# A five-branch decoder layer: the last product's pieces on two PSUM tiles, and one quarter of the last normalization

## Chip, cores and metric

The kernel runs on one core of one Trainium2 chip. The metric is the time of one execution on the device, in microseconds (us): the median of three runs of each kernel. Before the change it is 469.82 us (469.64 to 471.61).

## What is computed

One post-norm decoder layer over 256 tokens of width 1024. Five branches (block attention, a dilated-window mixture, forgetting attention, a gated delta rule, and cross-attention into 256 memory tokens) read the same input; each is gated, projected to width 1024 and merged under a sigmoid. What the change touches is the last of it:

```python
y = jnp.sum(jax.nn.sigmoid(merge_logits) * y, axis=2)   # (1, 256, 1024)
y = y @ w_out                                            # 1024 x 1024
return _layer_norm(DEEPNORM_ALPHA * x + y, ln_g, ln_b)

def _layer_norm(x, g, b):
    mu = x.mean(-1); var = square(x - mu).mean(-1)
    return (x - mu) * rsqrt(var + 1e-5) * g + b
```

All of it is float32. Each product is made of three matmuls: both operands are split into a rounded part (`hi`, by ScalarE) and a remainder (`lo`, by VectorE), and hi·hi, hi·lo and lo·hi are added up in PSUM (`mm3`, line 128 of the profile).

## The kernel before

The kernel goes through a list of weight units. Each unit loads a piece of a weight by DMA (line 176), splits it (lines 123 and 124) and multiplies it; small steps of the attention branches are dealt in between. The order on each engine is set when the kernel is built, by a scheduler that works from the program's order and a model of the time, and semaphores are set where one engine needs another's result.

The last product, `y @ w_out`, is done in `out_units`. Its output has two halves of 128 tokens, t = 0 and t = 1. They are cut into five **pieces** (`PC`): t = 0 into columns 0 to 511 (piece 0) and 512 to 1023 (piece 1); t = 1 into 0 to 511 (piece 2), 512 to 767 (piece 3) and 768 to 1023 (piece 4). Each piece adds up in its own PSUM space over 8 blocks of w_out's rows, k = 0 to 7. The blocks k = 0, 1, 2 are multiplied as they come, for all pieces in turn. The other five are kept back (`late`), and `finish` then multiplies them piece by piece: 15 matmuls for piece 0, 15 for piece 1, and so on. When a piece is complete, VectorE adds the residual to it and writes it to SBUF (line 1071, here called the eviction), and takes its mean and variance (line 1072). After the last piece of a half, `norm(t)` normalizes it: the statistics are brought together (1055), ScalarE takes a square root (1058), VectorE takes the reciprocal (1059), and for each half of the columns, c = 0 and 1, VectorE makes two passes over 128x512 elements (1062: subtract the mean, times g; 1063: times the reciprocal, plus b). Column half 0 then leaves by a DMA from SyncE's queue, column half 1 by one from ScalarE's queue (1064).

The PSUM space of the pieces: two tiles `lg` of two 512-column halves each, and one tile `mm` of 512 columns. Before the change pieces 0 and 1 are the two halves of the first `lg` tile (lg_6037 in the order below), pieces 2 and 3 those of the second (lg_6038), and piece 4 lies in `mm` (mm_6039). `big` in the profile is here the residual stream `xres`, written in place (big_4557), and the tile of g and b (big_4559).

Of the kernel before, what the change touches and what calls it, by code (L numbers as in the profile page):

```python
# [11 lines left out]
AF = mybir.ActivationFunctionType  # L12
ALU = mybir.AluOpType
AX = mybir.AxisListType

P = 128
# [60 lines left out]
def kernel(ctx: ExitStack, tc: tile.TileContext, T: dict, out: bass.AP):  # L77
    nc = tc.nc
# [8 lines left out]
    V_, A_, PE, G_ = nc.vector, nc.scalar, nc.tensor, nc.gpsimd  # L87
# [14 lines left out]
    def spt(tag, shape, dt=F32, bufs=None):  # L102
        return sp.tile(list(shape), dt, tag=tag, name=nm(tag), bufs=bufs)

    def ct(name, shape, dt=F32):
        return cpool.tile(list(shape), dt, name=name)

    def pst(tag, shape, bufs):
        return ps.tile(list(shape), F32, tag=tag, name=nm(tag), bufs=bufs)

    def mmps(shape=(P, S)):
        return pst("mm", shape, 3)

    def lgps():

        return pst("lg", (P, 2, 512), 2)
# [9 lines left out]
    def mm3(pt, lh, ll, rh, rl, first, last, pin=False):  # L126
        for l, r, start, stop in ((lh, rh, first, False), (lh, rl, False, False), (ll, rh, False, last)):
            ins = PE.matmul(pt, l, r, start=start, stop=stop)  # L128
            if pin:
                tc.keep_in_program_order(ins)  # L130
# [697 lines left out]
    st, mv, rstd = ct("st", (P, 2, 2, 6)), ct("mv", (P, 2, 2)), ct("rstd", (P, 2))  # L828
# [174 lines left out]
    fin = {}  # L1003
# [15 lines left out]
    def out_units():  # L1019

        PC = [((0, 512), (512, 1024)), ((0, 512), (512, 768), (768, 1024))]

        def out_mm(u, k, t, i, first, last):
            lo, hi = PC[t][i]
            ts = slice(t * P, (t + 1) * P)
            yh, yl = (y[:, k % 3, ts] for y in yhl[k // 3])
            if k > 5:
                h, l = (x[lo // 512][:, lo % 512:lo % 512 + hi - lo] for x in (u.h, u.l))
            else:
                h, l = u.h[:, lo:hi], u.l[:, lo:hi]  # L1030
            mm3(fin["p"][t][i][:, :hi - lo], yh, yl, h, l, first, last, pin=not first)

        def chunk(u, k, t):
            if k == 0 and t == 0:
                lgs = [lgps() for _ in range(2)]
                fin["p"] = [[lg[:, i] for i in range(2)] for lg in lgs]
                fin["p"][1].append(mmps((P, 512)))
                warm = spt("warm", (P, 1), bufs=1)
                A_.activation(warm, yhl[2][0][:, 1, 0:1].bitcast(F32), AF.Sqrt, scale=0.0, bias=0.0)
            if k < 3:  # L1040
                for i in range(len(PC[t])):
                    out_mm(u, k, t, i, k == 0, False)
            elif t == 0:
                late.append((u, k))

        for k in range(6):
            units.append(Unit(T["wo"][:, k * 1024:(k + 1) * 1024], 1024,
                              [lambda u, k=k: chunk(u, k, 0), lambda u, k=k: chunk(u, k, 1)]))

        def finish():  # L1050
            xres, lngb = R["xres"], R["lngb"]
            st2 = [ct(f"st{t}", (P, len(PC[t]), 6)) for t in range(2)]

            def norm(t):
                V_.bn_aggr(mv[:, t], st2[t].rearrange("p c s -> p (c s)"))  # L1055
                rs = rstd[:, t:t + 1]
                V_.tensor_scalar(rs, mv[:, t, 1:2], LN_EPS, None, op0=ALU.add)  # L1057
                A_.activation(rs, rs, AF.Sqrt)
                V_.reciprocal(rs, rs)
                for c, cs in enumerate((slice(0, 512), slice(512, 1024))):  # L1060
                    o = xres[:, t, cs]
                    V_.scalar_tensor_tensor(o, o, mv[:, t, 0:1], lngb[:, 0, cs], op0=ALU.subtract, op1=ALU.mult)  # L1062
                    V_.scalar_tensor_tensor(o, o, rs, lngb[:, 1, cs], op0=ALU.mult, op1=ALU.add)  # L1063
                    (nc.sync, nc.scalar)[c].dma_start(out[t * P:(t + 1) * P, cs], o)

            for t in range(2):
                for i, (lo, hi) in enumerate(PC[t]):
                    for x, (u, k) in enumerate(late):
                        out_mm(u, k, t, i, False, x == len(late) - 1)
                    o = xres[:, t, lo:hi]  # L1070
                    V_.scalar_tensor_tensor(o, fin["p"][t][i][:, :hi - lo], 0.5, o, op0=ALU.mult, op1=ALU.add)  # L1071
                    V_.bn_stats(st2[t][:, i], o)  # L1072
                norm(t)

        fin["finish"] = finish
# [137 lines left out]
```

## Time and profile before

| | us |
|---|---|
| median of three runs (lowest to highest) | 469.82 (469.64 to 471.61) |
| the profiled execution, its own time | 472.55 |
| its span, first to last instruction | 470.6 |
| TensorE busy in the span | 452.8 |
| VectorE busy | 333.6 |
| ScalarE busy | 268.5 |
| GpSimd busy | 31.0 |

The profiled execution took 1.95 us more than its span, and 2.73 us more than the median of the three runs. A busy time is a sum over the whole span; what a change in the last 25 us is worth is read in those 25 us. PE is TensorE, DVE VectorE, ACT ScalarE, POOL GpSimd, SP SyncE; PEld is TensorE's weight load.

### The profile page before, as it was taken

How to read it: one execution, taken by the hardware profiler on the slowest of the kernel's cores; microseconds unless marked ns; L12 is line 12 of the kernel's file. 1: busy time of each engine (PE TensorE's matmuls, PEld its weight loads, DVE VectorE, ACT ScalarE, POOL GpSimd, SP SyncE). 2: the span in 40 equal slices, each digit the busy share in tenths (PEclk: the TensorE clock that was granted, in tenths of full speed). 3: DMA queues.
4: the chain of work that ended last, by engine and by line, in shares of the span. 5: the costliest groups of instructions: out<-in, count | busy, mean ns of one | idle time of the engine just before them, and what ended most of it. 6: DMA issues, size and time to landing. Idle time of an engine off the chain costs nothing. (4 is left out here: it accounts for less than half of the span.)

```text
span 470.6 us, 10295 instructions
## 1 busy us (share of the span) xinstructions
PE 452.8 (96%) x4039; PEld 427.9 (91%) x4039; DVE 333.6 (71%) x757; ACT 268.5 (57%) x520; POOL 31.0 (7%) x36
## 2 busy tenths in 40 slices
PE   6999999999999999999999999999989999999993
PEld 3999998999999999999999989998989999999973
DVE  4799998786897554664655799885566666688656
ACT  5555585666666644543434986764675654576610
POOL 0000030010000000000000132000011221100000
PEclk9899999999999999999999999999989999999998
DMA  7996487646544545666434167463755446677202
GB/s 250 361 347 207 133 253 234 179 138 173 156 135 130 151 125 170 200 176 209 124 91 131 56 213 235 133 203 117 263 171 167 143 127 176 190 235 238 88 0 91
DMA packets 35051, 81.40 MB, mean 173 GB/s; under 512 B 8969, under 2 KB 17467, under 8 KB 34875
## 3 DMA queue, kind: packets, MB, share of 16 engines
q1 hardware_dynamic: 34715, 80.22, 55.5%
q8 instruction: 32, 0.52, 0.5%
q10 hardware_dynamic: 288, 0.52, 0.3%
q14 instruction: 16, 0.13, 0.1%
HBM read 79.37 MB, written 1.36 MB: 172 GB/s over the span
## 5 line engine op out<-in xcount | busy, mean ns | idle before, releaser
L124 DVE TENSOR_TENSOR lo<-raw,hi 128x1024 fp32r<-128x1024 f32 (+4 forms) x163 | 170.7, 1047 | 85.1 <-ACT hi L123 84.4
L128 PE MATMUL mm<-xhi,hi 128*128 128x256 f32 x776 | 220.8, 285 | 2.0 <-ACT hi L123 1.6
L128 PE MATMUL mm<-xhi,lo 128*128 128x256 f32 x776 | 217.2, 280 | 1.7 <-DVE lo L124 1.7
L128 PE MATMUL mm<-xlo,hi 128*128 128x256 f32 x776 | 217.3, 280 | 0.0
L123 ACT ACTIVATE hi<-raw 128x1024 fp32r<-128x1024 f32 (+4 forms) x163 | 146.7, 901 | 120.7 <-PE mm L128 102.7
L128 PEld LDWEIGHTS mm<-xhi,hi 128*128 128x128 f32 x776 | 147.0, 189 | 7.2 <-issue 3.5
L128 PEld LDWEIGHTS mm<-xhi,lo 128*128 128x128 f32 x776 | 146.4, 189 | 2.2 <-DVE lo L124 2.1
L128 PEld LDWEIGHTS mm<-xlo,hi 128*128 128x128 f32 x776 | 146.5, 189 | 0.5 <-issue 0.5
L128 PE MATMUL mm<-f,hi 128*128 128x256 f32 x240 | 45.4, 284 | 0.2 <-ACT th L976 0.2
L994 POOL TENSOR_TENSOR yacc<-yacc,yt 128x256 f32<-128x256 f32 x24 | 24.0, 998 | 280.0 <-DVE yt L993 270.4
L128 PEld LDWEIGHTS mm<-f,hi 128*128 128x128 f32 x240 | 36.9, 189 | 1.2 <-ACT th L976 0.8
L128 PE MATMUL mm<-f,lo 128*128 128x256 f32 x120 | 34.0, 283 | 0.1
L128 PEld LDWEIGHTS mm<-f,lo 128*128 128x128 f32 x120 | 22.6, 188 | 0.6 <-DVE lo L124 0.6
L128 PE MATMUL mm<-hi,xhi 128*128 128x384 f32 (+1 forms) x48 | 16.8, 372 | 3.0 <-ACT hi L123 2.5
L135 PE MATMUL lg<-f,f 64*128 64x256 f32 (+2 forms) x192 | 18.5, 354 | 0.0
L976 ACT ACTIVATE th<-mm,bcol 128x256 f32<-128x256 f32 x40 | 18.4, 461 | 0.0
L768 ACT ACTIVATE pr<-pr,mm 128x128 f32<-128x128 f32 (+1 forms) x36 | 15.9, 443 | 4.3 <-DVE mm L759 4.3
L128 PE MATMUL mm<-lo,xhi 128*128 128x384 f32 (+1 forms) x48 | 17.3, 360 | 0.4 <-DVE lo L124 0.4
L128 PE MATMUL mm<-hi,xlo 128*128 128x384 f32 (+1 forms) x48 | 17.0, 355 | 0.0
L752 DVE CUSTOM_DVE_ANT_0 pr<-lg,cst 128x128 f32<-128x128 f32 (+1 forms) x48 | 14.1, 353 | 3.8 <-PE lg L135 3.8
L993 DVE SCALAR_TENSOR_TENSOR yt<-th,mm 128x256 f32<-128x256 f32 x32 | 13.3, 417 | 4.1 <-ACT th L976 2.3
L705 ACT ACTIVATE f<-mm,bcol 128x256 f32<-128x256 f32 x33 | 15.1, 457 | 0.0
(221 smaller groups left out, 519.4 us busy)
## 6 DMA issues: line engine op xcount, KB each, us to landing
raw<-in_wf_dram SPq DMA_DIRECT2D x60, 512.0 KB, 4.4
raw<-in_wm_dram SPq DMA_DIRECT2D x40, 512.0 KB, 3.6
raw<-in_wb_dram SPq DMA_DIRECT2D x40, 192.0 KB, 2.6
raw<-in_wt_dram SPq DMA_DIRECT2D x12, 384.0 KB, 3.3
raw<-in_wo_dram SPq DMA_DIRECT2D x8, 512.0 KB, 5.5
gr<-gscr SPq DMA_DIRECT2D x12, 128.0 KB, 3.4
raw<-in_wcs_dram SPq DMA_DIRECT2D x3, 402.0 KB, 7.0
raw<-in_mem_dram SPq DMA_DIRECT2D x2, 512.0 KB, 4.0
```

The lines of the kernel that those rows point to most:

```text
L123: A_.activation(hi, src, AF.Copy)
L124: V_.tensor_tensor(lo, src, hi.bitcast(F32), op=ALU.subtract)
L128: ins = PE.matmul(pt, l, r, start=start, stop=stop)
L135: keep(PE.matmul(pt, l, r, start=start, stop=stop))
L705: A_.activation(R[name][:, m], p, AF.Identity, bias=b, scale=1.0 if scale is None else scale)
L752: V_.tensor_tensor_reduce(l[:, sl], pts[x][:, sl], mk[x][:, sl], 1.0, 3.0e38, ALU.add, ALU.min, mx[x][:, t, g:g + 1])
L768: A_.activation(l[:, sl], l[:, sl], AF.Exp, bias=mms[x][:, t:t + 1], scale=-1.0, accum_out=sm_[x][:, t, g:g + 1])
L976: A_.activation(th, p, AF.Tanh, bias=bcol[:, i:i + 1], scale=0.5)
L993: V_.scalar_tensor_tensor(yt, st_["th"], 1.0, st_["p"], op0=ALU.add, op1=ALU.mult)
L994: (V_ if last else G_).tensor_tensor(yacc[:, d], yacc[:, d], yt, op=ALU.add)
```

## The change

Two edits, both in `out_units`.

The first deals the pieces crosswise to the two `lg` tiles: piece 0 takes the first half of the first tile and piece 1 the first half of the second tile; piece 2 takes the second half of the first tile and piece 3 the second half of the second tile. Piece 4 stays in `mm`. The pieces, their matmuls and their order by piece are as before.

The second concerns column half 1 of token half 0, a quarter of the final normalization. VectorE no longer makes its two passes there. Instead VectorE computes `nmr`, minus the mean times the reciprocal, one number per token; ScalarE computes (x + eviction) times the reciprocal plus `nmr` by one Identity activation over 128x512; GpSimd multiplies that by g and adds b, in two passes over 128x512; ScalarE's queue then issues the DMA of that quarter, as before.

```diff
             if k == 0 and t == 0:
                 lgs = [lgps() for _ in range(2)]
-                fin["p"] = [[lg[:, i] for i in range(2)] for lg in lgs]
+                fin["p"] = [[lg[:, t_] for lg in lgs] for t_ in range(2)]
                 fin["p"][1].append(mmps((P, 512)))
...
                 V_.reciprocal(rs, rs)
                 for c, cs in enumerate((slice(0, 512), slice(512, 1024))):
                     o = xres[:, t, cs]
+                    if t == 0 and c == 1:
+                        nmr = ct("nmr", (P, 1))
+                        V_.tensor_scalar(nmr, rs, mv[:, t, 0:1], -1.0, op0=ALU.mult, op1=ALU.mult)
+                        A_.activation(o, o, AF.Identity, scale=rs, bias=nmr)
+                        G_.tensor_tensor(o, o, lngb[:, 0, cs], op=ALU.mult)
+                        G_.tensor_tensor(o, o, lngb[:, 1, cs], op=ALU.add)
+                        nc.scalar.dma_start(out[t * P:(t + 1) * P, cs], o)
+                        continue
                     V_.scalar_tensor_tensor(o, o, mv[:, t, 0:1], lngb[:, 0, cs], op0=ALU.subtract, op1=ALU.mult)
```

The numbers of the lines below the edits grow by 1 to 10: the eviction is line 1081 in the changed kernel, its statistics 1082, the two VectorE passes 1072 and 1073, the square root 1059, ScalarE's Identity 1067, GpSimd's passes 1068 and 1069.

TensorE at the seam between piece 0 and piece 1, before. The names are output tile <- the two operands, and the bracket names the engine whose semaphore the instruction waits for:

```order
L128 MATMUL lg_6037<-hi_6101,f_1001_5793 128x512 [waits Activation_49]
L128 MATMUL lg_6037<-lo_6102,f_1001_5793 128x512 [waits DVE_49]
L128 MATMUL lg_6037<-hi_6101,f_1002_5794 128x512
L128 MATMUL lg_6037<-f_996_5773,f_1041_5973 128x512 [waits DVE_49]
L128 MATMUL lg_6037<-f_998_5775,f_1041_5973 128x512
```

The same place after the change:

```order
L128 MATMUL lg_6037<-hi_6101,f_1001_5793 128x512 [waits Activation_49]
L128 MATMUL lg_6037<-lo_6102,f_1001_5793 128x512 [waits DVE_49]
L128 MATMUL lg_6037<-hi_6101,f_1002_5794 128x512
L128 MATMUL lg_6038<-f_996_5773,f_1041_5973 128x512
L128 MATMUL lg_6038<-f_998_5775,f_1041_5973 128x512
```

The first matmul of piece 1 now writes the other tile and waits for no engine. Before, it waited for VectorE; the wait now stands at the first matmul of piece 2 (the other half of piece 0's tile) and at the first of piece 3 (the other half of piece 1's), each one piece later than the eviction that it waits for.

VectorE from the eviction of piece 1 to the statistics of piece 2, before:

```order
L1071 SCALAR_TENSOR_TENSOR big_4557<-lg_6037,big_4557 128x512
L1072 BN_STATS st_6105<-big_4557 128x6
L1055 BN_AGGR mv<-st_6105 128x2
L1057 TENSOR_SCALAR rstd<-mv 128x1
L1062 SCALAR_TENSOR_TENSOR big_4557<-big_4557,mv,big_4559 128x512 x2
L1059 RECIPROCAL rstd<-rstd 128x1
L1071 SCALAR_TENSOR_TENSOR big_4557<-lg_6038,big_4557 128x512
L1063 SCALAR_TENSOR_TENSOR big_4557<-big_4557,rstd,big_4559 128x512 x2
L1072 BN_STATS st_6106<-big_4557 128x6
```

The same stretch of VectorE after:

```order
L1081 SCALAR_TENSOR_TENSOR big_4557<-lg_6038,big_4557 128x512
L1082 BN_STATS st_6105<-big_4557 128x6
L1056 BN_AGGR mv<-st_6105 128x2
L1058 TENSOR_SCALAR rstd<-mv 128x1
L1072 SCALAR_TENSOR_TENSOR big_4557<-big_4557,mv,big_4559 128x512
L1060 RECIPROCAL rstd<-rstd 128x1
L1073 SCALAR_TENSOR_TENSOR big_4557<-big_4557,rstd,big_4559 128x512
L1066 TENSOR_SCALAR nmr<-rstd,mv 128x1
L1081 SCALAR_TENSOR_TENSOR big_4557<-lg_6037,big_4557 128x512
L1082 BN_STATS st_6106<-big_4557 128x6
```

Two of the four 128x512 passes are gone, one 128x1 operation is new, and the remaining passes all stand ahead of the eviction of piece 2.

ScalarE at its end, after the change (before, the Identity was not there and the first DMA waited for VectorE):

```order
L123 ACTIVATE hi_6101<-raw_6057 128x1024 [waits DMAHW4_49,PE_49]
L1059 ACTIVATE rstd<-rstd 128x1 [waits DVE_49]
L1067 ACTIVATE big_4557<-big_4557,nmr,rstd 128x512 [waits DVE_49]
L1070 DMA out_dram<-big_4557 128x512 [waits Pool_49]
L1059 ACTIVATE rstd<-rstd 128x1 [waits DVE_49]
L1074 DMA out_dram<-big_4557 128x512 [waits DVE_49]
```

The DMA that waits for GpSimd's second pass stands ahead of the square root of token half 1.

## Rows read from the trace of the kernel before

**Rows 1.** The chain that ended last, in order of time: start, length, what.
```profile
450.82 0.70 DVE big L1071
...
458.72 0.70 DVE big L1071
...
463.35 0.44 DVE big L1071
...
466.88 0.66 DVEq L1209
```

**Rows 2.** Who waited for whom, 434 to 471: total, times, longest.
```profile
PEld lg L128 <- DVE big L1071: 2.4, 2, 1.2
PE lg L128 <- DVE big L1071: 1.6, 2, 0.8
```

**Rows 3.** Timeline of TensorE at the seams: start, length, line, instruction, idle before.
```profile
450.39 0.39 PE L128 MATMUL lg<-hi,f 128*128 128x512 f32 x1
451.56 1.66 PE L128 MATMUL lg<-f,f 128*128 128x512 f32 x6 [0.78 <-DVE big L1071]
453.06 0.40 PE L128 MATMUL lg<-hi,f 128*128 128x512 f32 x1
...
454.89 0.39 PE L128 MATMUL lg<-hi,f 128*128 128x512 f32 x1
455.12 1.52 PE L128 MATMUL lg<-f,f 128*128 128x512 f32 x6
456.48 0.39 PE L128 MATMUL lg<-hi,f 128*128 128x512 f32 x1
...
458.29 0.39 PE L128 MATMUL lg<-hi,f 128*128 128x512 f32 x1
459.46 0.97 PE L128 MATMUL lg<-f,f 128*128 128x256 f32 x6 [0.78 <-DVE big L1071]
460.28 0.28 PE L128 MATMUL lg<-hi,f 128*128 128x256 f32 x1
...
461.35 0.88 PE L128 MATMUL mm<-f,f 128*128 128x256 f32 x6
462.07 0.28 PE L128 MATMUL mm<-hi,f 128*128 128x256 f32 x1
```

**Rows 4.** Timeline of VectorE in the last 16 us.
```profile
455.32 0.69 DVE L1071 SCALAR_TENSOR_TENSOR big<-lg,big 128x512 f32<-128x512 f32 x1 [3.08 <-PE lg L128]
...
457.02 0.15 DVE L1057 TENSOR_SCALAR rstd<-mv 128x1 f32<-128x1 f32 x1
457.09 1.41 DVE L1062 SCALAR_TENSOR_TENSOR big<-big,mv,big 128x512 f32<-128x512 f32 x2
...
460.65 0.69 DVE L1072 BATCH_NORM_STATS2 st<-big 128x6 f32<-128x512 f32 x1
...
464.61 1.41 DVE L1062 SCALAR_TENSOR_TENSOR big<-big,mv,big 128x512 f32<-128x512 f32 x2
465.94 0.15 DVE L1059 RECIPROCAL rstd<-rstd 128x1 f32<-128x1 f32 x1
```

**Rows 5.** Costliest groups by shape, ScalarE: count, busy, mean ns.
```profile
L123 ACT ACTIVATE xhi<-raw 128x512 fp32r<-128x512 f32 x3 | 1.9, 620 | 1.3 <-DMA raw<-in_xT_dram 1.3
```

**Rows 6.** Timelines of GpSimd and VectorE: two adds, and VectorE under the first.
```profile
281.70 1.99 POOL L994 TENSOR_TENSOR yacc<-yacc,yt 128x256 f32<-128x256 f32 x1 [1.20 <-DVE yt L993]
376.96 0.74 POOL L994 TENSOR_TENSOR yacc<-yacc,yt 128x256 f32<-128x256 f32 x1 [2.91 <-DVE yt L993]
...
281.88 1.22 DVE L124 TENSOR_TENSOR lo<-raw,hi 128x1024 fp32r<-128x1024 f32 x1
283.01 0.48 DVE L697 SCALAR_TENSOR_TENSOR og<-lg,gnw,f 128x256 f32<-128x256 f32 x1
```

**Rows 7.** Timeline of ScalarE at the end; ACTq is its queue issuing a DMA.
```profile
464.73 0.20 ACT L1058 ACTIVATE rstd<-rstd 128x1 f32<-128x1 f32 x1 [7.32 <-DVE rstd L1057]
467.57 0.34 ACTq L1064 DMA_DIRECT2D out_dram<-big  x1
```

## The prediction

> **What bounds the kernel now.** I read the page first: TensorE is busy 452.8 of the span's 470.6 us (the table above), so the time is TensorE's stream plus what stands before and behind it. The chain that ended last says where it is not: near the end it leaves TensorE twice for an eviction of 0.70 us on VectorE, at 450.82 and at 458.72, comes back to TensorE each time, and leaves it for good with the eviction of piece 4 at 463.35 [rows 1]. In the view of who waited for whom the same two places stand as matmuls waiting twice for the eviction, 1.6 us in all by the matmuls, 2.4 us by the weight loads in front of them [rows 2]. The reader should see that a wait on the engine that bounds the kernel, with nothing later to absorb it, is worth its full length.
>
> Why it waits is in the timeline of TensorE [rows 3]. Pieces 0 and 1 share a tile, and piece 1's first matmul starts at 451.56, just after piece 0's eviction ended (450.82 + 0.70 = 451.52). Piece 2 goes to the other tile and starts at 455.12, 0.23 us after the last matmul of piece 1 began, although the eviction of piece 1 comes only at 455.32 [rows 4]. Piece 3 shares piece 2's tile and waits again. So it is the common tile that makes a piece wait, not the eviction as such.
>
> **Edit 1, crosswise pieces.** It adds and removes no instruction. The price of a seam without a wait is 455.12 - 454.89 = 0.23 us from start to start. With it, the first seam took 451.56 - 450.39 = 1.17 and the second 459.46 - 458.29 = 1.17, so 0.94 us is lost at each. The stream also starts slowly after a stop: the first six matmuls of piece 1 took 453.06 - 451.56 = 1.50 us against 456.48 - 455.12 = 1.36 for piece 2, 0.14 more; those of piece 3 took 460.28 - 459.46 = 0.82 against 462.07 - 461.35 = 0.72 for piece 4, 0.10 more [rows 3]. Sum: 2 x 0.94 + 0.14 + 0.10 = **2.12 us**. The bounds are the two totals of the wait view, 1.6 and 2.4 [rows 2]; I take my own figure because it counts from start to start, which is what the stream loses.
>
> The waits do not vanish, they move: piece 2 now waits for the eviction of piece 0, piece 3 for that of piece 1. Piece 2 would start at 455.12 - 1.08 = 454.04, when piece 0's eviction is 2.5 us old (451.52); piece 3 would start near 457.4, and piece 1's eviction starts at 455.32 - 1.08 = 454.24 and is over by 454.93. Both waits are met, with some 2.5 us in hand. The matmuls of blocks k = 0 to 2 also change tile in their turn; those are the same matmuls on the same weights, so I cost that at nothing.
>
> What is late next? The eviction of piece 4 moves from 463.35 to 461.23, and everything behind it is one chain on VectorE, ScalarE's square root and the last DMA; it moves as a whole if each engine is free in time. That is where edit 2 comes in.
>
> **Edit 2, the quarter of the normalization.** On VectorE it removes two 128x512 passes, about 1.41 us (the pairs in [rows 4]), and adds one 128x1 operation, 0.15 us by the 128x1 operation at 457.02. In the new time: eviction of piece 1 at 454.24, its TENSOR_SCALAR 1.70 later at 455.94, one pass (half of 1.41) from 456.01, the reciprocal at about 456.71, the second pass to about 457.5, `nmr` to about 457.65. The eviction of piece 2 is due at 458.72 - 1.08 = 457.64. VectorE is just free. Without edit 2 it would be some 1.4 us late there, but the evictions and statistics of pieces 2 and 3 (0.69 and 0.69 [rows 4], 0.44 as piece 4's eviction [rows 1], and as much for its statistics) fill only 2.3 of the 3.59 us until piece 4's eviction is due, so it would have all but caught up. The removed passes are therefore off the path, and I book edit 2 at **0 us** gained. The most they could give is 1.4 less the spare 1.3, or 0.1 us.
>
> What edit 2 adds lies on two idle engines. ScalarE: one Identity over 128x512. The trace shows no such Identity; the nearest row is a copy of that size, 0.62 us [rows 5], so from 457.7 to 458.3. GpSimd: two passes of 128x512, a size and a multiply that the trace doesn't show. An add of 128x256 takes 0.74 us with GpSimd to itself [rows 6]; twice the elements cost between 0.74 and 1.48 each. I take 1.48, so the pair ends at 458.4 + 2.96 = 461.36. The upper bound is the slowest add, 1.99 us for 128x256, doubled: 3.98 each.
>
> The new wait is on ScalarE's queue: the DMA of this quarter waits for GpSimd, and behind it stands the square root of token half 1, then the last DMA. By my figures the DMA is issued by 461.36 + 0.34 = 461.7 [rows 7]; the square root is due at 464.73 - 2.12 = 462.61, and since the reciprocal that reads it is due only at 465.94 - 2.12 = 463.82 [rows 4], it may start as late as 463.6. That is 1.9 us of cover. Its transfer leaves 3.7 us or more ahead of the last one (467.57 - 2.12 = 465.45), so it doesn't set the end. SyncE's queue keeps its two output DMAs, and nothing follows on GpSimd.
>
> Does GpSimd disturb VectorE or the reverse? The slow add of [rows 6] began at 281.70, ran under a VectorE subtraction with two SBUF inputs (281.88 to 283.10) and ended 0.59 us after it: it lost 1.25 us there. Its last part lay beside VectorE's pass at 283.01, which reads one input from PSUM, and neither was held up much (0.48 us). In the new time GpSimd works from 458.4 to 461.4, beside evictions (one input from PSUM) and statistics (one SBUF input); the next VectorE passes with two SBUF inputs come at 464.61 - 2.12 = 462.49. So I book no conflict.
>
> The Trainium skill, page "SBUF — State Buffer", section "Who interferes with whom", states that a VectorE instruction with two SBUF inputs and a GpSimd instruction that reads SBUF hold a shared port exclusively, so that the later one fully blocks; with at most one SBUF input they don't contend. By that rule the slow add is a blocked one, and the pair here would take 2.96 us as long as it ends before 462.49; the trace agrees as far as its 1.99 against 0.74 us goes. The skill's "Perfetto Trace Analysis", section "Optimizing Scalar/DVE Operations", warns from the same cause that moving work between these two engines might not help. That would be the third rival below.
>
> **The sum.** Profiled span 470.6 - 2.12 = 468.5; the profiled execution's 472.55 would be 470.4; the median of the runs shown, 469.82, would be **467.7 us**, 0.45% less. The profiled execution lies 2.73 us above that median; the seams are a matter of order, so I take the same 2.12 off both.
>
> **Rivals.**
> 1. The wait stays (0.05). If a piece waited for the eviction just before it for another reason than the tile, both seams would keep their 0.94 us: 469.8. If only the seam to piece 3 kept it, 1.03 of the gain would go: 468.7. Against it: piece 2's free start at 455.12 [rows 3].
> 2. More than I count (0.09). The weight loads lose 1.2 us per seam [rows 2]; if that is what the stream loses, the gain is 2.4: 467.4. For it: loads run ahead of the matmuls; against it: start to start I find 2.12.
> 3. GpSimd holds ScalarE's queue (0.06); this one ends slower. If both passes cost their upper bound, the pair takes 7.96 us and ends at 458.4 + 7.96 = 466.36, the DMA issue lasts to 466.70, the square root to 466.90, and the reciprocal comes at 466.94, not 463.82: 3.12 us late, against a gain of 2.12. That is 470.8, 1.0 us slower than before. It costs nothing until the pair is longer than 463.6 - 0.34 - 458.4 = 4.9 us, and eats the gain at 7.0. For it: the 1.99 us add; against it: VectorE has no pass with two SBUF inputs beside the pair unless the pair is late already.
>
> **Chances and range.** The forecast has 0.80. A measurement of this kernel can tell about 0.5% from no change: 2.35 us, so "faster" begins at 467.47, only 0.23 us under the forecast. Two of the runs before differ by 0.18 and the third is 1.8 higher, so I give the forecast about 1 in 3 to fall beyond that line: 0.80 x 0.31 + 0.09 = 0.34 faster. Slower begins at 472.2, beyond rival 3's end: 0.03. The rest, 0.63, is no difference that can be told. The range takes rival 2 with a run's spread of some 0.7 below it, 466.7, and reaches over the bound of 1.6 (468.2) and a kept seam (468.7) to 469.0 above; it leaves out rival 3 and both seams kept.
>
> **What would show it.** Right: no matmul of the last stretch waits for an eviction; 45 matmuls of pieces 0 to 2 start at 0.23 us each; the eviction of piece 4 comes about 2.1 us nearer to piece 0's than 463.35 - 450.82 = 12.53, so at 10.4; GpSimd's two passes take about 1.5 each, and the square root of token half 1 follows its TENSOR_SCALAR at once. Wrong: an idle stretch before piece 1's first matmul (rival 1); the square root waiting for the DMA ahead of it, or VectorE's reciprocal idle before it (rival 3); a tail from piece 4's eviction to the last DMA longer than the 467.57 - 463.35 = 4.22 us of before.

## The result: slower, though the last stretch gained what was forecast

The changed kernel took 475.34 us in the median (473.51 to 476.31), the kernel before 471.53 (469.64 to 472.51), each over six runs side by side. The ratio is 1.0074, 95% interval 1.0049 to 1.0098: 0.7% slower, where 0.45% faster was forecast.

The chain of waits of the changed kernel, its last part (start, length, what). It answers to [rows 1]:

```profile
451.76 12.02 PE lg L128 x60
463.78 1.81 PE mm L128 x15
465.59 0.02 issue
465.61 0.43 DVE big L1081
...
469.14 0.66 DVEq L1219
```

The chain no longer leaves TensorE for an eviction: 60 matmuls of pieces 0 to 3 stand in one stretch. The list of who waited for whom has no row of TensorE waiting for line 1081, which answers to [rows 2]. The seam between pieces 0 and 1, from the timeline of TensorE, answers to the first two rows of [rows 3]:

```profile
454.80 0.39 PE L128 MATMUL lg<-hi,f 128*128 128x512 f32 x1
455.02 0.39 PE L128 MATMUL lg<-f,f 128*128 128x512 f32 x1
```

0.22 us from start to start, against 1.17. VectorE, ScalarE and GpSimd in the same last stretch, one timeline each (answering to [rows 4], [rows 7] and [rows 6]):

```profile
455.23 0.69 DVE L1081 SCALAR_TENSOR_TENSOR big<-lg,big 128x512 f32<-128x512 f32 x1 [1.11 <-PE lg L128]
...
461.91 0.21 DVE L1066 TENSOR_SCALAR nmr<-rstd,mv 128x1 f32<-128x1 f32 x1
462.04 0.68 DVE L1081 SCALAR_TENSOR_TENSOR big<-lg,big 128x512 f32<-128x512 f32 x1
...
465.61 0.42 DVE L1081 SCALAR_TENSOR_TENSOR big<-mm,big 128x256 f32<-128x256 f32 x1 [0.91 <-PE mm L128]
```

```profile
462.15 0.82 ACT L1067 ACTIVATE big<-big,nmr,rstd 128x512 f32<-128x512 f32 x1 [1.44 <-DVE nmr L1066]
465.73 0.38 ACTq L1070 DMA_DIRECT2D out_dram<-big  x1
466.99 0.20 ACT L1059 ACTIVATE rstd<-rstd 128x1 f32<-128x1 f32 x1 [4.02 <-DVE rstd L1058]
469.84 0.34 ACTq L1074 DMA_DIRECT2D out_dram<-big  x1
```

```profile
463.05 1.28 POOL L1068 TENSOR_TENSOR big<-big,big 128x512 f32<-128x512 f32 x1 [49.61 <-ACT big L1067]
464.41 1.28 POOL L1069 TENSOR_TENSOR big<-big,big 128x512 f32<-128x512 f32 x1
```

From the eviction of piece 0 to that of piece 4 it is 465.61 - 455.23 = 10.38 us, against 463.35 - 450.82 = 12.53 before: 2.15 us gained. From there to the last DMA it is 4.23, against 4.22. So the tail did as forecast. But piece 0's eviction itself comes at 455.23 instead of 450.82, 4.41 us late, and no edit lies ahead of it. 4.41 - 2.15 = 2.26 is the difference of the two spans (472.9 - 470.6 = 2.3).

Where the 4.41 us arise is seen in the longest piece of the chain, the last 396 matmuls of the body. First before, then after:

```profile
393.21 45.80 PE mm L128 x396
```

```profile
396.18 47.24 PE mm L128 x396
```

The same 396 matmuls (288 of x with a weight, 108 of a branch output with a weight) take 47.24 us instead of 45.80, with no wait in either: 0.1193 us each instead of 0.1157. The timeline of TensorE shows it in single matmuls (start, length, ...). Before:

```profile
436.08 0.28 PE L128 MATMUL mm<-xhi,hi 128*128 128x256 f32 x1
436.20 0.28 PE L128 MATMUL mm<-xlo,hi 128*128 128x256 f32 x1
...
436.99 0.28 PE L128 MATMUL mm<-xhi,lo 128*128 128x256 f32 x1
437.10 0.28 PE L128 MATMUL mm<-xhi,hi 128*128 128x256 f32 x1
```

After, the same kind of matmul:

```profile
440.40 0.28 PE L128 MATMUL mm<-xhi,hi 128*128 128x256 f32 x1
440.52 0.28 PE L128 MATMUL mm<-xlo,hi 128*128 128x256 f32 x1
...
441.35 0.28 PE L128 MATMUL mm<-xhi,lo 128*128 128x256 f32 x1
441.47 0.28 PE L128 MATMUL mm<-xhi,hi 128*128 128x256 f32 x1
```

The nine steps took 1.02 us before (0.113 each) and 1.07 after (0.119). The length of a matmul, 0.28, says nothing here; the distance from start to start does. I set the two lists of starts, one matmul against the same one, up to piece 0: the 2,223 steps in which x is multiplied by a weight and no wait lies (under 0.14 us in both) lost 6.08 us together; the 105 longer steps among them gave back 1.69; the other 1,650 steps added up to 0.02.

The granted clock was not lower, 0.992 of full in the mean against 0.988. But not all of the 1.69 us are waits. In the profiled execution of before, TensorE's clock fell to half (1.2 GHz) from 343.4 to 346.8 us, after an idle stretch of 1.56 us; the x-times-weight matmuls there started 0.213 us apart. The first line is from the view of busy time by stretch (the 0.50 is the clock), the others from the timeline of TensorE:

```profile
343.40:346.80 3.40, 3.23 (x14) 2.83 (x14) 2.38 (x6) 3.32 (x5) 0.73 (x1) 0.50 0.35 83
...
343.16 0.39 PE L128 MATMUL mm<-xhi,hi 128*128 128x256 f32 x1 [1.56 <-ACT hi L123]
...
345.12 0.41 PE L128 MATMUL mm<-xlo,hi 128*128 128x256 f32 x1
345.33 0.41 PE L128 MATMUL mm<-xhi,lo 128*128 128x256 f32 x1
```

The changed kernel idled as long at the same place and kept the full clock. That is worth 1.02 of the 1.69 us, and no edit made it. So 4.41 us is what this pair of executions shows; by the medians the body lost more: 475.34 - 471.53 = 3.81, and 2.15 gained at the end, make about 6.0 us.

Why should x times a weight be slower? The one thing that the change does to the body is not an instruction. `nmr` is created in the pool of constants, which lies in SBUF ahead of the pools of raw, hi, lo, f3 and big. Its one number per partition takes 32 bytes there (by the addresses in the built program), so all tiles behind it move by 32 bytes: hi from 90816 to 90848, while xhi stays at 16512. That was **theory A**: the place of the tiles costs the body its time. **Rival B**: one of the two edits itself slows the body. **Rival C**: the body differs from build to build or run to run, whatever is in it.

### The profile page after: what moved, and what is told of

It is laid out like the page before. It is cut to its first block, busy times and chain, and to the rows that moved or that the text cites. A ratio compares the mean times of both kernels' runs of the same rounds, so it can differ in the third digit from the quotient of the medians.

```text
span 472.9 us, 10302 instructions
## 1 busy us (share of the span) xinstructions
PE 457.0 (97%) x4039; PEld 432.8 (92%) x4039; DVE 332.9 (70%) x756; ACT 269.8 (57%) x521; POOL 32.4 (7%) x38
## 5 line engine op out<-in xcount | busy, mean ns | idle before, releaser
L994 POOL TENSOR_TENSOR yacc<-yacc,yt 128x256 f32<-128x256 f32 x24 | 22.8, 949 | 284.8 <-DVE yt L993 275.1
```

Of the source, the lines that this page charges most:

```text
L994: (V_ if last else G_).tensor_tensor(yacc[:, d], yacc[:, d], yt, op=ALU.add)
```

## Experiments: which part of the change slows the body

Four kernels, timed against the kernel before on one and the same chip.

**The 32 bytes alone.** The kernel before, plus an unused tile where `nmr` stood:

```diff
             st2 = [ct(f"st{t}", (P, len(PC[t]), 6)) for t in range(2)]
+            pad = ct("pad", (P, 1))
```

> The kernel before, with nothing added but a tile of one number per partition that no instruction uses, created where the changed kernel creates nmr. It takes 32 bytes in each partition and moves the tiles behind it (raw, hi, lo, f3, big and the rest) by 32 bytes, as nmr does; xhi and xlo stay. Theory A (the place of the tiles costs the body of the kernel): in the changed kernel the stream of 128x256 matmuls ran 0.1180 us apart where before it ran 0.1153, 4.4 us over the body, so about +4.4 us on the kernel before, 0.9% slower, with the last 25 us as before. Rival B (one of the two edits itself slows the body): no change, within 0.2%. Rival C (the body differs from build to build or run to run): any value, not bound to the 32 bytes.

Measured: ratio 1.0118 (1.0088 to 1.0148); 478.15 us against 472.56. The chain of this kernel:

```profile
395.97 47.24 PE mm L128 x396
451.55 3.44 PE lg L128 x15
...
455.76 7.13 PE lg L128 x30
```

The long piece is 47.24, to the digit that of the changed kernel, and the seams (455.76 after 451.55 + 3.44) still stop as before. An unused tile costs 1.2%. The 0.9% expected, which came from one pair of profiled executions, lies at the edge of the interval. The next run takes the 32 bytes away again.

**Both edits, no tile moved.**

```diff
-                        nmr = ct("nmr", (P, 1))
+                        nmr = spt("nmr", (P, 1), bufs=1)
```

> The changed kernel, with both edits, but nmr is taken from the last pool, so that it lies behind all other tiles and every other tile lies where it lay before. Theory A: the loss in the body is gone and the 2.1 us of the tail stay, so 0.45% faster than before. Rival B: as the changed kernel, 0.7% slower. Rival C: anything between.

Measured: 0.9960 (0.9934 to 0.9986); 470.62 us. Its chain:

```profile
392.14 45.80 PE mm L128 x396
...
446.28 12.02 PE lg L128 x60
```

The body is back at 45.80 and the seams are gone. This kernel and the changed one have the same instructions in the same order on every engine, and they differ by 1.1% (0.9960 against 1.0074) through the place of four bytes.

**Edit 1 alone.**

```diff
-                fin["p"] = [[lg[:, i] for i in range(2)] for lg in lgs]
+                fin["p"] = [[lg[:, t_] for lg in lgs] for t_ in range(2)]
```

> Edit 1 alone: the pieces dealt crosswise, the normalization as before, no new tile. Theory A: the seams' 2.1 us are gained and no more than 0.1 us of it is lost to VectorE, so 0.43 to 0.45% faster than before. Rival B, if it is the crosswise tiles that slow the body: 0.4 to 0.9% slower.

Measured: 0.9955 (0.9933 to 0.9977); 469.77 us. This is the forecast's gain from one line; with an interval of 0.2% to either side, that it agrees to the decimal is luck. VectorE at its end in this kernel:

```profile
459.97 0.43 DVE L1072 BATCH_NORM_STATS2 st<-big 128x6 f32<-128x256 f32 x1
460.58 0.42 DVE L1071 SCALAR_TENSOR_TENSOR big<-mm,big 128x256 f32<-128x256 f32 x1 [0.19 <-PE mm L128]
```

Though it makes all four passes of token half 0, VectorE is idle 0.19 us before piece 4: it has caught up, and edit 2 has nothing to give.

**Edit 2 alone**, with `nmr` from the last pool, as above.

> Edit 2 alone: the quarter on ScalarE and GpSimd, the pieces on the tiles as before, nmr taken from the last pool so that no other tile moves. Theory A and the prediction: no difference (within 0.1%), since the passes lay beside TensorE's work. Rival B, if it is the work on ScalarE and GpSimd that slows the body: 0.7 to 1.1% slower.

Measured: 1.0008 (0.9985 to 1.0031); 472.96 us: no difference. The long piece is 45.80 here too:

```profile
392.31 45.80 PE mm L128 x396
```

Rival B falls in both halves. Rival C falls with it: the kernel before and three more builds with the tiles in the same place took 45.80 us for those 396 matmuls, and two builds with the 32 bytes took 47.24. (Executions do differ, by stretches at half clock as the one above; none of these long pieces has one in it.)

## Experiments: what about the place matters

Three theories were left; they were tried on two other chips, four kernels on each, again with the kernel before beside them. A1: the weights' tile has to start at a multiple of 64 bytes (it did before, and doesn't after). A2: what matters is the distance between the two operands. A3: both have to start at multiples of 64. From one k to the next x moves by 1024 bytes and the weight by 512, so their distance modulo 512 is the same for all these matmuls: 64 before, 96 after.

**All tiles moved by 32 together**, x and weights: distance 64.

```diff
+    pad = ct("pad", (P, 1))
     xhi, xlo = ct("xhi", (P, KD, S), F32R), ct("xlo", (P, KD, S), F32R)
```

> The kernel before, with an unused tile of 32 bytes created ahead of xhi, so that all tiles move by 32 bytes together: x and the weights' hi and lo both lie at 32 modulo 64, and their distance is as before (64 modulo 512). Theory A1 (a matmul reads slower when the tile of its weights doesn't start at a multiple of 64 bytes): about 1% slower, as with 32 bytes behind x. Theory A2 (what matters is the distance between the two operands): as before, within 0.2%.

Measured: 1.0015 (0.9995 to 1.0035), and 45.80 for the long piece:

```profile
393.98 45.80 PE mm L128 x396
```

Weights at 32 modulo 64, and no loss: A1 and A3 fall.

**x at 32, weights at 0 modulo 64**: distance 96.

```diff
+    padx = ct("padx", (P, 1))
     xhi, xlo = ct("xhi", (P, KD, S), F32R), ct("xlo", (P, KD, S), F32R)
...
             st2 = [ct(f"st{t}", (P, len(PC[t]), 6)) for t in range(2)]
+            pad = ct("pad", (P, 1))
```

> The kernel before, with 32 unused bytes ahead of xhi and 32 more ahead of raw: x lies at 32 modulo 64, the weights' hi and lo at 0 modulo 64, at a distance of 96 modulo 512, which is the distance in the changed kernel. Theory A1 (the place of the weights): as before, within 0.2%. Theory A2 (the distance): about 1% slower. Theory A3 (both operands have to start at multiples of 64): about 1% slower; the run with all tiles moved parts A2 from A3.

Measured: 1.0126 (1.0095 to 1.0158), long piece 47.24:

```profile
397.42 47.24 PE mm L128 x396
```

The same distance as the changed kernel at other addresses, and the same loss.

**The changed kernel with `nmr` on 64 bytes**, the repair that A1 would suggest: distance 128.

```diff
-                        nmr = ct("nmr", (P, 1))
+                        nmr = ct("nmr", (P, 16))[:, 0:1]
```

> The changed kernel with nmr cut from a tile of 16 numbers, 64 bytes instead of 4, so that the tiles behind it move by 64: x and weights both at 0 modulo 64, distance 128 modulo 512. Theories A1 and A3: the body as before and the tail 2.1 us shorter, 0.45% faster. Theory A2: another pace, as likely 0.7% slower.

Measured: 1.0134 (1.0105 to 1.0163), worse than the changed kernel.

**Edit 1 with 192 unused bytes**: distance 256.

```diff
+            pad = ct("pad", (P, 48))
```

> Edit 1 alone with 192 unused bytes ahead of raw: both operands at 0 modulo 64, distance 256 modulo 512. Theories A1 and A3: 0.45% faster than before, as edit 1 alone. Theory A2: another pace than at a distance of 64, faster or slower; if the stream found its quick pace always, up to 4 us more gain (2,200 matmuls at 0.1133 instead of 0.1153 us), 1.3% faster.

Measured: 1.0158 (1.0127 to 1.0188). Both operands at multiples of 64, and a greater loss than at 96: it is the distance, not the alignment, that goes with the loss. Four more kernels looked for a better one, each edit 1 with an unused tile of 448, 480, 416 or 384 bytes at the same place (distances 0, 32, 480 and 448). The first:

```diff
             st2 = [ct(f"st{t}", (P, len(PC[t]), 6)) for t in range(2)]
+            pad = ct("pad", (P, 112))
```

> Edit 1 alone with unused bytes ahead of raw, so that the weights lie at a distance of 0 modulo 512 from x. Distances measured so far, with the mean spacing of x-times-weight matmuls: 64 at 115.3 ns, 96 at 118.1, 128 at 118.7, 256 at 119.8. Theory A2 as it stands says only that the distance decides. If the pace falls off to both sides of 64, about 118 ns: 0.9% slower than edit 1 alone, 0.4 to 0.6% slower than before. If it is best at 0: faster than edit 1 alone, up to 1.3% faster than before. Against the latter: the branch outputs times weights, at a distance of 0 in all kernels, ran 118 to 120 ns apart.

Measured: 1.0114 (1.0075 to 1.0154).

> As the run at 0, at a distance of 32 modulo 512; here the weights lie at 32 modulo 64. If 64 is a peak in the pace: about 118 ns, 0.5% slower than before. If the pace only grows worse from 0 upwards: 114 ns or less, 0.8 to 1.3% faster than before.

Measured: 1.0059 (1.0038 to 1.0080).

> As the run at 0, at a distance of 480 modulo 512, or minus 32. If the pace falls off to both sides of 64, 118 to 120 ns: 0.5 to 1.5% slower than before. If it depends on the distance up from the weights to x in a ring of 512, anything between.

Measured: 1.0005 (0.9984 to 1.0027).

> As the run at 0, at a distance of 448 modulo 512, or minus 64. If what counts is how far apart the two are, whichever is ahead: as edit 1 alone, 115.3 ns and 0.45% faster than before. If it counts which is ahead: 118 to 120 ns, 0.5 to 1.5% slower than before.

Measured: 1.0039 (1.0005 to 1.0072).

None is better than edit 1 alone, 0.9955. All distances in one table; the step is the mean from the start of a 128x256 matmul of x with a weight to that of the next such, steps over 0.14 us left out, some 2,200 in each trace, and the long piece is the chain's 396 matmuls:

| distance modulo 512 | kernels | step, ns | long piece, us |
|---|---|---|---|
| 0 | edit 1 + 448 bytes | 119.8 | 47.70 |
| 32 | edit 1 + 480 bytes | 118.3 | 47.08 |
| 64 | before; edit 1; edit 2; both; all moved | 115.3 to 115.5 | 45.80 |
| 96 | changed; before + 32 bytes; x at 32 | 118.0 to 118.2 | 47.24 |
| 128 | `nmr` on 64 bytes | 118.7 | 47.30 |
| 256 | edit 1 + 192 bytes | 119.8 | 47.70 |
| 448 | edit 1 + 384 bytes | 117.6 | 47.15 |
| 480 | edit 1 + 416 bytes | 117.3 | 47.05 |

Four of the long pieces, in the order 256, 0, 448, 480, each from its kernel's chain:

```profile
399.56 47.70 PE mm L128 x396
```

```profile
401.58 47.70 PE mm L128 x396
```

```profile
395.30 47.15 PE mm L128 x396
```

```profile
394.43 47.05 PE mm L128 x396
```

By the step, 64 is the best of the eight distances, with a fall to both sides, though not evenly: 480 is nearer to it than 32 or 96 are. The expectations for single runs came out less well. At 32 the 0.5% expected were 0.6; at 0 the loss was larger than the 0.4 to 0.6% expected; at 480, where a fall to both sides of 64 was put at 0.5 to 1.5% slower, the time was that of the kernel before; and at 448 it was 0.4% slower (0.05 to 0.72), against the 0.45% faster of one guess and short of the 0.5 to 1.5% slower of the other. The time follows the step only roughly: at 480 some 2,200 steps, each 1.9 ns longer than in edit 1 alone, make 4.2 us, and the profiled spans differ by 470.9 - 467.8 = 3.1. The kernels at 0 and 256 have the same step and long piece and ratios of 1.0114 and 1.0158. That the kernel before stands at the best of the eight was not arranged by anything in its code. What in the memory or in TensorE makes the distance count stays open: no run here parts the read of x from the load of the weight. Nor were other distances tried, and in these runs all tiles behind the constants moved together, so the table is one of this kernel's layout, and that it is the weight's distance from x, and not that of another tile, is argued and not shown.

Two things in the same traces limit it. The tiles of the branch outputs moved together with the weights, so the 108 matmuls of the two in the long piece keep their distance in all kernels; and yet their mean step is 117.8 to 117.9 ns in the kernels at 64, 118.7 to 118.8 at 96 and 120.0 at 0 and 256: how far apart a matmul's own operands lie is not all that counts. And where x is the stationary operand (the 128x384 matmuls, 91 steps under 0.2 us), the step is 173.5 ns at 64 and 176.5 at 96, but 173.9 at 0 and at 256, where the table has its worst.

## Why the prediction was wrong, point by point

- **The seams** (edit 1): right, in the mechanism and in the size. 2.12 us were forecast; the last stretch gained 2.15, and edit 1 alone made the kernel 0.45% faster, as the sum said. (The share of the second seam in rival 1, 1.03, should be 0.94 + 0.10 = 1.04; nothing hangs on it.)
- **Edit 2 gains nothing**: right. Alone it is at 1.0008 (0.9985 to 1.0031), with edit 1 at 0.9960 against 0.9955 without it, and the trace of edit 1 alone shows VectorE catching up with 0.19 us to spare.
- **The moved waits and ScalarE's queue**: right. GpSimd's passes took 1.28 each (1.48 taken), the Identity 0.82 instead of the 0.62 of a copy, and `nmr` 0.21 instead of 0.15. The DMA issue was over at 465.73 + 0.38 = 466.11, and the square root started at 466.99, right behind its TENSOR_SCALAR. Less the 4.41 us that the body came late, the issue was over at 461.70, the forecast's 461.7: the Identity's 0.20 too little and the passes' 0.20 each too much came near to cancelling, which is luck. Rival 3 did not come about, nor did rivals 1 and 2.
- One reading of [rows 6] is not right: the add of 0.74 us did not have GpSimd "to itself". VectorE's subtraction with two SBUF inputs began 0.38 us after it, and it was the subtraction that took longer, 1.44 us against the 1.22 at 281.88. So an add beside it can cost VectorE as well. It didn't matter here, since no such pass stood beside the pair. The line is from the timeline of VectorE before:

```profile
377.34 1.44 DVE L124 TENSOR_TENSOR lo<-raw,hi 128x1024 fp32r<-128x1024 f32 x1 [0.46 <-ACT hi L123]
```

- **The step that failed** is "adds one 128x1 operation, 0.15 us": the operation was costed and its result's place was not. From that followed the sum, which took 2.12 us off a body held to be unchanged. What the runs showed in its place: the 32 bytes that `nmr` takes slow the body, by 4.41 us in the profiled pair, by about 6.0 in the medians, and by 478.15 - 472.56 = 5.59 with the unused tile alone. No rival covered it, so the range ended at 469.0; the lengths it took for single instructions were off by 0.2 us at most, and that did not help.
- **The range** had a second fault. It was set on a median of three runs, 469.82; the later medians of the same kernel were 471.53 to 472.71. The kernel that gained just what was forecast, edit 1 alone, took 469.77 us, which lies outside 466.7 to 469.0. So the time would probably have missed the range even with the body unchanged.
- It could have been seen, though not priced. The added line `ct("nmr", (P, 1))` names the first pool, and a tile added there moves every pool behind it. No row of the trace before says that this costs time. What the trace did hold is a stream that runs at two paces with the same instructions: x-times-weight matmuls 0.113 us apart at 436 us, and 0.118 in the mean of the 285 that start at 19.1 us.

The faster kernel is the one with edit 1 alone, 0.9955 of before; with edit 2 added at no cost in place it is 0.9960, the same within the intervals.

## What to carry to other kernels

A new tile is an edit to every tile allocated behind it: when a change adds one, compare the addresses in the two built programs, and put it behind the tiles that the bounding engine reads. When a part that wasn't edited gets slower, compare start to start there before looking for a wait; here no wait view showed anything. And when two edits go together, time each alone: one line of this change was worth all the gain, and the other brought the loss through four bytes.

## What was unexpected of the hardware

- In this kernel the spacing of float32r 128x256 matmuls with a weight load each, x as the moving operand, goes with how far apart the two operands' addresses are: 115.3 ns at a distance of 64 modulo 512, 118 at 32 or 96, 119.8 at 0 or 256. Here, where TensorE bounds the time, that is up to 2% of it (0.9955 against 1.0158, both edit 1).
- At a distance of 64 the stream has two paces, about 113.5 and 118 ns, and keeps one for dozens of matmuls; in the trace before, 59% of the steps with `hi` lay under 114.5 ns, at a distance of 96 none did. In the traces the pace changes where the stream stops or where matmuls with other operands come between, not within an unbroken run of x-times-weight matmuls, but for a few slower steps at its ends. What selects it was not tested.
- The Trainium skill, page "SBUF — State Buffer", section "Who interferes with whom", says that only the port shared by VectorE and GpSimd causes contention and that TensorE never waits on anyone. For the two engines these traces agree: GpSimd's two passes took 1.28 us each beside evictions and statistics, and the subtraction at 377.34, which began after an add, took 1.44 us instead of 1.22. For TensorE they add something: no row shows it waiting for another engine in the long piece, and yet the place of the tiles alone changes its pace, 45.80 against 47.24 us. Which of its reads slows was not shown.
